# The entry of the gate-and-up stage in another order

## The chip, the core and the metric

The kernel runs on one core of one Trainium2 chip. The metric is the device time of one execution in microseconds (us), the median over several runs. TensorE (PE in the profile) multiplies, VectorE (DVE), ScalarE (ACT) and GpSimd (POOL) do the rest, and transfers are issued by the SyncE queue (SP) and by the POOL queue. The profile writes L1218 for line 1218 of the kernel.

## The reference

Two layers of a streaming encoder over 512 tokens of width 1024. Each layer is a mixer and a dense SwiGLU network, each followed by a residual and a layer norm. The change touches the second half alone, which runs once per layer:

```python
def swiglu_ffn(x, w_gate_up, w_down):
    gu = x @ w_gate_up
    gate, up = gu[..., :FFN_HIDDEN], gu[..., FFN_HIDDEN:]
    return (jax.nn.silu(gate) * up) @ w_down

x = layer_norm(DN_ALPHA * x + h, ln_g[i, 0], ln_b[i, 0])
x = layer_norm(DN_ALPHA * x + swiglu_ffn(x, w_gate_up[i], w_down[i]), ln_g[i, 1], ln_b[i, 1])
```

FFN_HIDDEN is 2816. Everything is in float32.

## The kernel before

**Split operands.** Every float32 operand is cut in two parts, a rounded one (h) and the rest (l), and a product is the sum h·h + h·l + l·h, three matmuls. `split` (L190 to L193) does it in two instructions: ScalarE rounds (`CAST`, L191), VectorE subtracts (`TENSOR_TENSOR`, L192). Each split therefore costs both engines one pass, and the matmuls with l wait for VectorE.

**Gate and up as seven products.** `ffn` (from L1121) multiplies x by the gate and up weights for six groups of 512 or 384 columns. x is seen as 2 by 2 blocks (first and second half of the tokens, first and second half of the 1024 inputs), and so are the weights (gate and up, halves of the inputs). Seven block products P1 to P7 take the place of eight, with sums of blocks on both sides. On the x side P1, P2 and P4 read blocks of x itself, and P3, P5, P6 and P7 read sums of them. `place` and `A` say where each lies: P1, P2, P4 and P7 in the tiles xh and xl, and P5, P6 and P3 in Sh and Sl.

**The sums of x.** Each token tile of 128 is turned by TensorE (`Norm.turn`, L1022) after its layer norm. The first two token tiles (t 0 and 1) are the first half: `keep` (L1153) copies what was turned into float32 tiles called full. In the first layer `again` (L1156) turns those two tiles a second time for that. The other two (t 2 and 3) are the second half: `sink` takes what was turned straight out of PSUM, and for each of them (u is 0 or 1) it makes four VectorE sums (L1177, L1179, L1180, L1184) and five splits (P3, P4, P7, P5, P6). All nine VectorE instructions and five casts are recorded inside the turn.

**The sums of the weights.** These are made by transfers that add into SBUF: `more` (L1245) issues them on the POOL queue, two of 512 KB after the splits of P1, P3, P7 and P6. P3 reads the tile Y, then a block is added to Y and P7 reads it, then another for P6, then another for P4. So P3, P7, P6 and P4 of one group form a chain: split, transfer, split, transfer. The tiles Z and those of the next groups come by the SP queue (L1241).

**A product** (`product`, L1206; its matmuls are L1218) is done in two halves of two input blocks: each half is one split of 128x1024 and twelve matmuls of 512 columns, eight with h and then four with l. The split parts go into a ring of two tiles (wh, wl). Every third half from P3 of the first group on goes into a further pair named third, made at `parts`:

```python
        if spare and count[0] % 3 == 0:
            if not third:
                third.extend(hid.make(4 + r, "third", F32R).rearrange("p m s -> p (m s)") for r in range(2))
```

It lies where `whole(1)` has its full tiles (hid 4 and 5). So the first split into third, the first half of P3 of the first group, comes after the last instruction that reads those full tiles.

**The order by hand.** `work` (L1312) sets the order of the products. G0 is the first group, G1 the second. Before the change: G0 P1 (`begin`, L1308), then the turns with their sums, then G1 P1, G0 P2, G1 P2, G0 P3, P7, P5, P6, then G0 P4, the turn of G0's first result (`turn(0)`, transposes L1296 and copies L1297), G1 P3, G0's second turn, G1 P7, P5, P6. At G0's P6 the results are combined on VectorE (`dve`, L1252): eight instructions that lead to the operand of `turn(0)`.

**What sorts the instructions.** The order of recording is not the order of running. The framework gives each engine its list: of the instructions whose inputs are ready by its own estimate of times, the one that was recorded first goes next. On the chip each list is then run strictly in turn. So the change moves recording positions, and the lists follow where readiness lets them.

**The two entries.** Layer 0 enters at L1735 to L1743 (about 415 to 484 us of the span), where turns 2 and 3 stand in the code of the body. Layer 1 enters through `down_ln` (L1036), which calls `g.between` between the last norm's scale and the last turn (about 1047 to 1115 us).

Of the kernel before, what the change touches and what calls it, by code (L numbers as in the profile page):

```python
# [13 lines left out]
ALU = mybir.AluOpType  # L14
# [3 lines left out]
P = 128  # L18
# [171 lines left out]
def split(nc, h, l, src, eng=None):  # L190
    c = nc.scalar.copy(h, src)  # L191
    (eng or nc.vector).tensor_tensor(l, in0=src, in1=h, op=ALU.subtract)  # L192
    return c  # L193
# [895 lines left out]
def run(gen):  # L1089
    while True:  # L1090
        try:
            next(gen)
        except StopIteration as e:
            return e.value
# [26 lines left out]
def ffn(g, i, hid, ep):  # L1121
# [7 lines left out]
    nc = g.nc  # L1129
# [8 lines left out]
    def place(t, S_, name):  # L1138
        return {"P1": t[:, :4, :256], "P2": t[:, 4:, :256], "P4": t[:, 4:, 256:], "P7": t[:, :4, 256:],
                "P5": S_[:, 0], "P6": S_[:, 1], "P3": S_[:, 2]}[name]  # L1140

    A = {n: (place(xh, Sh, n), place(xl, Sl, n)) for n in ("P1", "P2", "P3", "P4", "P5", "P6", "P7")}
# [3 lines left out]
    def whole(u):  # L1146
        if u not in full:
            t = [hid.make(i, "full") for i in ((4, 5) if u else (3,))]
            rows = [t[i // 3][:, i % 3] if u else t[0][:, i] for i in range(4)]
            full[u] = {n: r.rearrange("p (k t) -> p k t", t=P) for n, r in zip(("P1", "P2", "P7", "P6"), rows)}  # L1150
        return full[u]

    def keep(u, q, p):  # L1153
        nc.scalar.copy(whole(u)["P2" if q else "P1"], p)

    def again(x):  # L1156

        for u in range(2):
            for q in range(2):
# [3 lines left out]
                    nc.tensor.transpose(out=p[:, i * P:(i + 1) * P], in_=x[:, u, k * P:(k + 1) * P], identity=g.C("ident"))  # L1163
                keep(u, q, p.rearrange("p (j t) -> p j t", t=P))

    def sink(t, q, p):
        if t < 2:
            keep(t, q, p)
            return False
        u = t % 2  # L1170
        f = whole(u)

        def out(n, src):
            split(nc, *(A[n][r][:, :, P * u:P * u + P] for r in range(2)), src)

        if q == 0:
            nc.vector.tensor_tensor(f["P7"], in0=f["P1"], in1=p, op=ALU.subtract)  # L1177
        else:
            nc.vector.tensor_tensor(f["P6"], in0=p, in1=f["P7"], op=ALU.add)  # L1179
            nc.vector.tensor_tensor(f["P2"], in0=f["P6"], in1=f["P2"], op=ALU.subtract)  # L1180
            out("P3", f["P2"])
            out("P4", p)
            out("P7", f["P7"])
            nc.vector.tensor_tensor(f["P1"], in0=f["P6"], in1=f["P1"], op=ALU.subtract)  # L1184
            out("P5", f["P1"])
            out("P6", f["P6"])
        return True


    third = []  # L1190
# [110 lines left out]
    gs = [group(j) for j in range(len(GROUPS))]  # L1301
# [3 lines left out]
            for x in gs[:2]:  # L1305
                x.load(k)

    def begin():  # L1308

        gs[0].step("P1", False)  # L1310

    def work():  # L1312

        gs[1].step("P1", False)
        gs[0].step("P2", False)
        gs[1].step("P2", False)
        last = len(gs) - 1
        for j, x in enumerate(gs):
            more = j < 4
            if j:  # L1320
                if j > 1:
                    x.step("P1", more)
                gs[j - 1].step("P4", more)
                gs[j - 1].turn(0)
            x.step("P3", more)
            if j:
                gs[j - 1].turn(1)
            if j > 1:
                x.step("P2", more)
            if 0 < j < last:  # L1330
                gs[j + 1].load("Z")
                gs[j + 1].load("X")
                gs[j + 1].load("Y")
            x.step("P7", more)
            x.step("P5", more)
            x.step("P6", more)
        gs[last].step("P4", False)
        return [lambda h=h: gs[last].turn(h) for h in range(2)]
# [328 lines left out]
def body(tc, I, O, coff, voff, dbg=False):  # L1667
    nc = tc.nc
    g = Ctx()
# [3 lines left out]
    with ExitStack() as es:  # L1673
# [30 lines left out]
        def dump(n):  # L1704
            if dbg:
                nc.sync.dma_start(O[n].rearrange("(t p) d -> p t d", p=P), x)
# [3 lines left out]
        def down(hid, i, li, left, beside=None, **kw):  # L1710

            late = 4
            S_ = g.tp.tile([P, 4 * late, S], F32R, name="late")

            def rows(n, kb):
                if beside:
                    beside.step(1)
                if n == 0 and kb == 2:
                    for f in left:
                        f()  # L1720
                i_ = kb - (NH // 2 - late)
                if n and i_ >= 0:
                    hl = [(S_[:, 4 * i_ + q], S_[:, 4 * i_ + 2 + q]) for q in range(2)]
                else:
                    h, l = (g.tp.tile([P, 1024], F32R, tag=t, name=t, bufs=2) for t in ("ah", "al"))
                    hl = [(h[:, 512 * q:512 * q + 512], l[:, 512 * q:512 * q + 512]) for q in range(2)]
                for q in range(2):
                    g.copied = split(nc, *hl[q], hid.row(2 * kb + q))
                return hl

            run(down_ln(g, I[f"w_dn{i}"], NH, rows, x, li, late=late, park=hid.park, **kw))

        with tc.tile_pool(name="tp1", reuse_waits="tile", bufs=1) as tp:
            hid = Hidden(tp)
            with tc.tile_pool(name="tu1", reuse_waits="tile", bufs=1) as g.tp:  # L1735
                f = ffn(g, 0, hid, tp)
                f.load()
                f.begin()
                f.again(x)
                g.sink = f.sink  # L1740
                g.norm.turn(2)
                g.norm.scale(3)
                g.norm.turn(3)  # L1743
                g.sink = None
                dump("x0")
                left = f.work()
            with tc.tile_pool(name="td1", reuse_waits="tile", bufs=1) as g.tp:
                rope = Background(rope_tables(g))
                down(hid, 0, 1, left, rope)
                tabs = rope.finish()  # L1750
            dump("x1")
# [4 lines left out]
        with tc.tile_pool(name="tp3", reuse_waits="tile", bufs=1) as tp:  # L1756
            hid = Hidden(tp)
            with tc.tile_pool(name="tu3", reuse_waits="tile", bufs=1) as g.tp:
                f = ffn(g, 1, hid, tp)
                g.sink = f.sink  # L1760

                def places(i):
                    if i:
                        return hid.park(i - 1)
                    return [tuple(tp.tile([P, S], F32R, tag="e", name="park", bufs=10) for r in range(2)) for q in range(2)]

                g.park = places
                g.between = lambda: (f.load(), f.begin())
                run(down2)
                g.sink = None  # L1770
                dump("x2")
                left = f.work()
            with tc.tile_pool(name="td3", reuse_waits="tile", bufs=1) as g.tp:
                down(hid, 1, 3, left, final=O["out"])
# [17 lines left out]
```

## Time and profile before

| | |
|---|---|
| median of 3 runs | 1410.62 us (1406.97 to 1412.29) |
| the profiled execution | 1414.36 us, span 1412.6 us |
| TensorE matmuls busy | 1348.7 us, 95% of the span |
| VectorE busy | 950.4 us, 67% |
| ScalarE busy | 652.9 us, 46% |
| GpSimd busy | 261.2 us, 18% |
| moved by transfers | 153.46 MB |

The span is the time from the first to the last instruction in the trace. A row of the timeline gives the start, the duration, the engine and line, the tile written and the tile read, and in brackets the idle time just before it with what ended it.

### The profile page before, as it was taken

What the parts mean: (1) busy time and instruction counts of PE and PEld (TensorE: products, weight loads), DVE (VectorE), ACT (ScalarE), POOL (GpSimd) and SP (SyncE); (2) the same over time, 40 slices, a digit from 0 to 9 for tenths busy, and PEclk for the clock granted to TensorE, in tenths of its full rate; (3) what the DMA queues carried; (4) which work ended last, traced back from release to release, by engine and by line L of the source; (5) the groups of instructions that cost most, each with busy time, mean ns of one, the idle gap of its engine ahead of it and who ended that gap; (6) DMA issues with size and microseconds to landing.
All of it is one profiled execution on the core that took longest, in us unless ns stands there. A gap on an engine that the chain in (4) does not pass through costs nothing.

```text
span 1412.6 us, 21622 instructions
## 1 busy us (share of the span) xinstructions
PE 1348.7 (95%) x8382; PEld 1067.9 (76%) x8382; DVE 950.4 (67%) x1720; ACT 652.9 (46%) x1114; POOL 261.2 (18%) x276
## 2 busy tenths in 40 slices
PE   7989999999899999999999999999999999999997
PEld 4767767766577788898887877666677788997886
DVE  3588867754586677668456457888796666667556
ACT  6533234254336455455343255555545455555341
POOL 1533112322321111126401230000001111120000
PEclk9999999999899999999999999999999999999999
DMA  5212111110458698773323212121267688763232
GB/s 188 75 56 58 35 39 39 57 39 24 141 224 164 156 197 170 155 138 87 100 96 107 96 58 78 43 66 45 90 179 177 153 191 160 158 125 96 90 108 86
DMA packets 66264, 153.46 MB, mean 109 GB/s; under 512 B 20336, under 2 KB 21488, under 8 KB 66032
## 3 DMA queue, kind: packets, MB, share of 16 engines
q1 hardware_dynamic: 51808, 103.83, 22.4%
q0 software_dynamic: 13824, 46.14, 19.2%
q10 hardware_dynamic: 528, 2.10, 0.4%
q8 instruction: 66, 1.08, 0.3%
q14 instruction: 38, 0.31, 0.1%
HBM read 149.09 MB, written 2.95 MB: 108 GB/s over the span
## 4 chain that ended last, share of the span: by engine, by line
PE 66%; DVE 13%; issue 10%; DMA 6%; ACT 2%; POOL 1%; DVEq 0%; POOLq 0%; ACTq 0%; SPq 0%
PE ps_g L1218 14%; PE ps_g L185 12%; PE ps_g L186 12%; PE ps_g L187 11%; DMA raw<-in_w_gu 5%; PE ps_s L1595 3%; PE ps_o L1624 2%; PE ps_t L1611 1%; PE ps_c L696 1%; POOL raw L1245 1%; DVE x L1014 1%; DVE pr L630 1%; PE ps_c L655 1%; PE ps_c L185 1%; DVE wl L192 1%
## 5 line engine op out<-in xcount | busy, mean ns | idle before, releaser
L192 DVE TENSOR_TENSOR wl<-raw,wh 128x1024 fp32r<-128x1024 f32 (+1 forms) x116 | 127.6, 1110 | 88.1 <-ACT wh L191 86.0
L191 ACT CAST wh<-raw 128x1024 fp32r<-128x1024 f32 (+1 forms) x116 | 111.5, 965 | 139.0 <-PE ps_g L1218 93.2
L1245 POOL DMA_DIRECT2D raw<-in_w_gu x96 | 83.2, 870 | 496.8 <-DVE wl L192 398.5
L213 POOL TENSOR_TENSOR wl<-w,wh 128x512 fp32r<-128x512 f32 x64 | 89.7, 1405 | 249.0 <-ACT wh L212 201.5
L1218 PE MATMUL ps_g<-wh,xh 128*128 128x512 f32 (+1 forms) x312 | 116.6, 374 | 2.1 <-ACT wh L191 2.1
L185 PE MATMUL ps_g<-xh,wh 128*128 128x512 f32 (+2 forms) x296 | 117.1, 396 | 0.0
L1218 PE MATMUL ps_g<-wh,xl 128*128 128x512 f32 (+1 forms) x312 | 115.4, 370 | 0.0
L187 PE MATMUL ps_g<-xh,wl 128*128 128x512 f32 (+2 forms) x296 | 114.4, 386 | 0.0
L186 PE MATMUL ps_g<-xl,wh 128*128 128x512 f32 (+2 forms) x296 | 114.3, 386 | 0.0
L186 PE MATMUL ps_g<-wl,ah 128*128 128x512 f32 x288 | 112.0, 390 | 0.6 <-DVE wl L192 0.6
L185 PE MATMUL ps_g<-wh,ah 128*128 128x512 f32 x288 | 111.6, 392 | 0.8 <-ACT ah L191 0.6
L192 DVE TENSOR_TENSOR wl<-w,wh 128x1024 fp32r<-128x1024 f32 (+2 forms) x79 | 89.6, 1134 | 31.7 <-ACT wh L191 31.3
L187 PE MATMUL ps_g<-wh,al 128*128 128x512 f32 x288 | 110.8, 389 | 0.0
L191 ACT CAST wh<-w 128x1024 fp32r<-128x1024 f32 (+3 forms) x85 | 80.5, 951 | 64.0 <-PE ps_g L186 36.1
L192 DVE TENSOR_TENSOR al<-hid,ah 128x512 fp32r<-128x512 f32 x72 | 49.3, 696 | 60.5 <-ACT ah L191 60.4
L191 ACT CAST ah<-hid 128x512 fp32r<-128x512 f32 x72 | 43.5, 618 | 98.9 <-PE ps_g L186 98.9
L1218 PE MATMUL ps_g<-wh,Sh 128*128 128x512 f32 (+1 forms) x232 | 85.7, 369 | 0.0
L1218 PE MATMUL ps_g<-wh,Sl 128*128 128x512 f32 (+1 forms) x232 | 85.0, 367 | 0.0
L1218 PE MATMUL ps_g<-wl,xh 128*128 128x512 f32 (+1 forms) x312 | 78.8, 374 | 3.3 <-DVE wl L192 3.3
L212 ACT CAST wh<-w 128x512 fp32r<-128x512 f32 x64 | 39.6, 618 | 90.2 <-PE ps_g L186 56.0
L185 PEld LDWEIGHTS ps_g<-xh,wh 128*128 128x128 f32 (+1 forms) x296 | 57.0, 192 | 14.7 <-issue 5.3
L1218 PEld LDWEIGHTS ps_g<-wh,xh 128*128 128x128 f32 x312 | 59.1, 190 | 11.2 <-ACT wh L191 3.5
(458 smaller groups left out, 3266.8 us busy)
## 6 DMA issues: line engine op xcount, KB each, us to landing
raw<-in_w_gu POOLq DMA_DIRECT2D x64, 512.0 KB, 5.6
w<-in_w_dn SPq DMA_DIRECT2D x44, 512.0 KB
raw<-in_w_gu SPq DMA_DIRECT2D x32, 512.0 KB
w<-in_w_even SPq DMA_DIRECT2D x48, 256.0 KB
raw<-in_w_gu POOLq DMA_DIRECT2D x32, 384.0 KB, 4.9
w<-in_w_gu SPq DMA_DIRECT2D x12, 512.0 KB
raw<-in_w_gu SPq DMA_DIRECT2D x16, 384.0 KB
w<-in_w_q SPq DMA_DIRECT2D x12, 384.0 KB
```

Source lines behind the costliest of these rows:

```text
L185: nc.tensor.matmul(out, lhsT=wh, rhs=xh, start=first, stop=False)
L186: nc.tensor.matmul(out, lhsT=wh, rhs=xl, start=False, stop=False)
L187: nc.tensor.matmul(out, lhsT=wl, rhs=xh, start=False, stop=last)
L191: c = nc.scalar.copy(h, src)
L192: (eng or nc.vector).tensor_tensor(l, in0=src, in1=h, op=ALU.subtract)
L212: nc.scalar.copy(h, w)
L213: nc.gpsimd.tensor_tensor(l, in0=w, in1=h, op=ALU.subtract)
L630: nc.vector.tensor_tensor(pr[:, :r, :r], in0=Ti[:, :r, :r].rearrange("p s j -> p j s"), in1=bc(e.N[:, :r, r].unsqueeze(1), [64, r, r]), op ...
L1218: nc.tensor.matmul(acc[u][:, :n], lhsT=A_[a][:, k, P * u:P * u + P], rhs=w[:, q], start=first and k + a + b == 0, stop=k + b == 4, skip_gr ...
L1245: nc.gpsimd.dma_start(T[k][k2], w[r, q, k2], accum_op=ALU.add)
L1595: nc.tensor.matmul(p[:, :nk], lhsT=Q[:, h % 4, qb * P:(qb + 1) * P], rhs=K[:, h % 4, :nk], start=True, stop=True)
L1624: nc.tensor.matmul(o[64 * e:64 * e + 64, kb * P:], lhsT=Vv[:, kb, (h - 1 + e) * 64:(h + e) * 64], rhs=t[e][kb][:, kb * P:], start=kb == 0, ...
```

## The change

Three edits. In `sink`, the turn of token tiles 2 and 3 makes only what reads the transposes (sums L1177 and L1179, and the split of P4). The other two sums and four splits go to a new function `sums`, which `work` calls in two places: P3's after G0 P2, those of P7, P5 and P6 after G1 P2. Then G1 P1 is recorded earlier, between the last norm's scale and the last turn. Last, for G0 alone, `turn(0)` is recorded after G1 P3 in place of before it. No instruction is added or left out.

```diff
+    def out(u, n, src):
+        split(nc, *(A[n][r][:, :, P * u:P * u + P] for r in range(2)), src)
+
     def sink(t, q, p):
...
         if q == 0:
             nc.vector.tensor_tensor(f["P7"], in0=f["P1"], in1=p, op=ALU.subtract)
         else:
             nc.vector.tensor_tensor(f["P6"], in0=p, in1=f["P7"], op=ALU.add)
-            nc.vector.tensor_tensor(f["P2"], in0=f["P6"], in1=f["P2"], op=ALU.subtract)
-            out("P3", f["P2"])
-            out("P4", p)
-            out("P7", f["P7"])
-            nc.vector.tensor_tensor(f["P1"], in0=f["P6"], in1=f["P1"], op=ALU.subtract)
-            out("P5", f["P1"])
-            out("P6", f["P6"])
+            out(u, "P4", p)
         return True
+
+    def sums(*names):
+        for n in names:
+            for u in range(2):
+                f = whole(u)
+                o = {"P3": "P2", "P5": "P1"}.get(n, n)
+                if o != n:
+                    nc.vector.tensor_tensor(f[o], in0=f["P6"], in1=f[o], op=ALU.subtract)
+                out(u, n, f[o])
...
-    def begin():
-
-        gs[0].step("P1", False)
+    def begin(n):
+
+        gs[n].step("P1", False)

     def work():

-        gs[1].step("P1", False)
         gs[0].step("P2", False)
+        sums("P3")
         gs[1].step("P2", False)
+        sums("P7", "P5", "P6")
...
                 gs[j - 1].step("P4", more)
-                gs[j - 1].turn(0)
+                if j > 1:
+                    gs[j - 1].turn(0)
             x.step("P3", more)
             if j:
-                gs[j - 1].turn(1)
+                for h in range(0 if j == 1 else 1, 2):
+                    gs[j - 1].turn(h)
...
-                f.begin()
+                f.begin(0)
                 f.again(x)
                 g.sink = f.sink
                 g.norm.turn(2)
                 g.norm.scale(3)
+                f.begin(1)
                 g.norm.turn(3)
...
-                g.between = lambda: (f.load(), f.begin())
+                g.between = lambda: (f.load(), f.begin(0), f.begin(1))
```

## Rows read from the trace of the kernel before

**Rows 1.** The page, part 1: busy time by engine.

```profile
PE 1348.7 (95%) x8382; PEld 1067.9 (76%) x8382; DVE 950.4 (67%) x1720; ACT 652.9 (46%) x1114; POOL 261.2 (18%) x276
```

**Rows 2.** Windows: busy of PE, PEld, DVE, ACT, POOL, then PEclk, DMA share, GB/s.

```profile
430.00:435.00 5.00, 2.92 (x13) 2.06 (x11) 5.00 (x8) 3.15 (x5) 0.00 (x0) 1.00 0.84 155
...
475.00:480.00 5.00, 4.09 (x20) 3.51 (x21) 5.00 (x8) 2.17 (x4) 1.34 (x2) 1.00 0.25 43
...
1065.00:1070.00 5.00, 4.59 (x21) 3.43 (x19) 5.00 (x9) 4.27 (x7) 0.00 (x0) 1.00 1.02 311
1070.00:1075.00 5.00, 3.51 (x9) 2.79 (x10) 4.93 (x5) 3.48 (x5) 0.86 (x1) 0.70 0.42 171
```

**Rows 3.** TensorE's waits, 400 to 520 us: total, times, longest.

```profile
PE ps_g L1218 <- ACT third L191: 3.0, 2, 2.2
PE ps_s L1296 <- DVE w L1252: 2.5, 2, 1.3
```

**Rows 4.** TensorE's waits, 1030 to 1160 us.

```profile
PE ps_g L1218 <- DVE wl L192: 3.1, 3, 1.9
PE ps_s L1296 <- DVE w L1252: 1.7, 2, 1.2
PE ps_g L1218 <- ACT third L191: 1.0, 1, 1.0
```

**Rows 5.** The first entry, timeline: third's release, its split, what follows.

```profile
434.06 1.04 ACT L191 CAST third<-raw 128x1024 fp32r<-128x1024 f32 x1 [1.18 <-DVE Sl L192]
...
435.15 0.50 PE L1218 MATMUL ps_g<-third,Sh 128*128 128x512 f32 x1 [2.24 <-ACT third L191]
...
436.22 1.21 DVE L192 TENSOR_TENSOR third<-raw,third 128x1024 fp32r<-128x1024 f32 x1
...
437.96 0.86 POOL L1245 DMA_DIRECT2D raw<-in_w_gu  x1 [1.41 <-PE ps_g L1218]
...
438.49 1.21 DVE L192 TENSOR_TENSOR wl<-hid,wh 128x1024 fp32r<-128x1024 f32 x1
...
447.84 1.05 ACT L191 CAST wh<-raw 128x1024 fp32r<-128x1024 f32 x1 [3.88 <-DMA raw<-in_w_gu]
...
450.71 0.39 PE L1218 MATMUL ps_g<-wh,xh 128*128 128x512 f32 x1
```

**Rows 6.** The chain that ended last: adding transfers (start, us, what).

```profile
437.96 9.78 DMA raw<-in_w_gu
...
450.45 5.33 DMA raw<-in_w_gu
...
477.19 5.30 DMA raw<-in_w_gu
```

**Rows 7.** The first entry, timeline: from G0's results to G1's P7.

```profile
470.87 1.28 DVE L1252 TENSOR_TENSOR u<-ps_g,s 128x512 f32<-128x512 f32 x2
...
475.68 1.22 DVE L192 TENSOR_TENSOR wl<-raw,wh 128x1024 fp32r<-128x1024 f32 x1
...
482.57 1.04 ACT L191 CAST third<-raw 128x1024 fp32r<-128x1024 f32 x1 [3.81 <-DMA raw<-in_w_gu]
...
483.67 0.50 PE L1218 MATMUL ps_g<-third,xh 128*128 128x512 f32 x1 [0.78 <-ACT third L191]
```

**Rows 8.** The second entry, timeline: P2's splits, third, what follows.

```profile
1052.13 1.17 DVE L192 TENSOR_TENSOR wl<-raw,wh 128x1024 fp32r<-128x1024 f32 x1
...
1071.49 1.64 PE L1218 MATMUL ps_g<-wl,xh 128*128 128x512 f32 x4 [1.90 <-DVE wl L192]
...
1072.58 1.23 DVE L192 TENSOR_TENSOR third<-raw,third 128x1024 fp32r<-128x1024 f32 x1
...
1074.11 0.86 POOL L1245 DMA_DIRECT2D raw<-in_w_gu  x1 [11.42 <-DVE third L192]
...
1079.58 1.05 ACT L191 CAST wh<-raw 128x1024 fp32r<-128x1024 f32 x1 [1.66 <-DMA raw<-in_w_gu]
...
1082.31 0.39 PE L1218 MATMUL ps_g<-wh,xh 128*128 128x512 f32 x1
```

More of the change, by code (lines that the diff above doesn't have):

```diff
@@ L1171, in sink @@
         f = whole(u)
-        def out(n, src):
-            split(nc, *(A[n][r][:, :, P * u:P * u + P] for r in range(2)), src)
         if q == 0:
```

## The prediction

> **What bounds the kernel now.** I read the page first: TensorE's matmuls fill 95% of the span [rows 1], so time is won only where TensorE stands still. Then TensorE's waits in the two stretches that the change touches. In the first entry it waits 3.0 us for third and 2.5 us for the operand of the first turn [rows 3]; in the second 3.1 us for split weights, 1.7 us for that operand and 1.0 us for third [rows 4]. Next the windows, to see who was late: VectorE is busy for 5.00 of 5.00 us around 430 and 1065 us, and nearly so after 1070 [rows 2]. It is the engine behind there. One more loss stands in those rows: after TensorE's wait of 1.90 us [rows 8] its granted clock is 0.70 on average, between its levels of 1.2 and 2.4 GHz, so it spent part of that window at the lower. Nine matmuls take 3.51 us there, 0.39 each, against 4.59 / 21 = 0.22 in the window before [rows 2]: 9 x 0.17 = 1.5 us.
>
> Last the chain that ended last, which shows what waits behind VectorE: the adding transfers [rows 6]. A split that ends on VectorE lets POOL issue a transfer, which takes 5.3 us or, once, 9.78 us, and only then can the next product of that group be split. In G0 these links follow each other with nothing but G0's own products between.
>
> **The sums later, G1's P1 earlier.** Nothing is added or dropped; four of nine VectorE instructions per token tile are the two sums and two splits of P3 and P5, two more the splits of P7 and P6: twelve over both tiles, some 0.64 us each by the nearest pair of that size (two in 1.28 [rows 7]), move behind the splits of P2. In the first entry the wait of 2.24 us at 435.15 [rows 5] goes, since the splits of G1 P1 and G0 P2 no longer stand behind those twelve. TensorE would then reach G0 P7 at 450.71 - 2.24 = 448.47.
>
> What is late next is third. Its tiles hold the sums' inputs, so its split must follow all twelve, as its cast already followed them before [rows 5]. VectorE was full up to it, and three P2 splits ran after it (one of them is the 438.49 row [rows 5]). They are now recorded ahead of it and should run first, as the sums are no longer there to hold them up. So third's split ends at 437.43 + 3 x 1.21 = 441.06 in place of 437.43. From that end to the transfer's issue it was 0.53 us, from landing to the cast 0.10, the cast 1.05 [rows 5, 6]. With a transfer of 5.33 us G0 P7's first half is ready at 441.06 + 0.53 + 5.33 + 0.10 + 1.05 = 448.07, just ahead of TensorE at 448.47. The transfer is the unknown: its bounds are 5.30 and 9.78 [rows 6]. I take 5.33, because two of three rows lie there. The gain is 2.24 us.
>
> In the second entry the waits of 3.1 us [rows 4] and the 1.5 us of clock would go, and TensorE would be at G0 P7 at 1082.31 - 4.6 = 1077.7. But there all P2 splits ran before third already (1071.49 waits for the last but one, third follows at 1072.58 [rows 8]). VectorE has the same work ahead of third and was full, so third still ends at 1072.58 + 1.23 = 1073.81, the transfer is issued at 1074.11, and P7's cast runs from 1079.58 to 1080.63. TensorE waits 2.9 us more and starts P7 at 1080.63 in place of 1082.31: a gain of 1.68 us, with 2.9 of the 4.6 us turned into a wait for the transfer.
>
> Moves at no cost: the twelve casts (ScalarE has 3.15 of 5.00 us in use [rows 2]; if that cover went, one cast, 0.6 us). G1 P1 takes its two adding transfers with it, but the turn that it passes issues none on POOL or SP, so POOL's order stays G0 P1, G1 P1, G0 P3. Its copies go to banks of its own.
>
> **The first turn later.** The waits for its operand are 2.5 and 1.7 us [rows 3, 4]. I cost the move at nothing. VectorE makes eight combinations from 470.87 on, and only then, at 475.68, the split of G1 P3; that split's end starts the transfer at 477.19, 5.30 us, on which G1 P7 waits at 483.67 [rows 6, 7]. Moving the transposes leaves these VectorE instructions where they are, so TensorE gets G1 P3's matmuls with h earlier and then waits longer for its l parts and for P7. The bounds: both waits won, 4.2 us; or the later waits for third, 0.78 [rows 7] and 1.0 [rows 4], once more, a loss of 1.8. I take zero, as the chain through 475.68 and 477.19 is the nearest. Whatever G0 gains ahead of P6 shifts that chain as a whole, so the 2.24 and 1.68 us stay.
>
> **Sum.** 2.24 + 1.68 + 0 = 3.92 us: 1414.36 becomes 1410.4. The profiled execution lies 3.7 us above the median shown, so in medians 1410.6 becomes 1406.7.
>
> A rule against the change: adding transfers are issued by POOL while VectorE is full. The transfer at 477.19 took 5.30 us with VectorE busy for 5.00 of 5.00 us [rows 2, 6], as long as the others, so the sum charges nothing for it. The Trainium skill (SBUF — State Buffer, section Who interferes with whom) says that a VectorE instruction with two SBUF inputs contends with a GpSimd instruction that reads SBUF. By that rule each of the two transfers could stand behind one split more, an estimate of 2 x 1.2 = 2.4 us, and the sum would be a gain of 1.5; the trace does not show it.
>
> **Rivals.** (1) *All waits go.* The lists are sorted anew; where P7 is not ready, products that are (G0 P5, G1 P3) may be put ahead of it, and the turn's transposes fill the rest. Then 3.0 + 2.5 in the first entry and 3.1 + 1.7 + 1.0 + 1.5 in the second are won [rows 2 to 4], 12.8 us: 1397.8, or about 1401 with three quarters of it. For it: the list takes whatever is ready first. Against it: in both entries the order G0 P3, P7 was kept before while ScalarE stood idle 3.88 and 1.66 us for P7's transfer [rows 5, 8].
>
> (2) *The adding transfer stretches*, and the change is slower. Place: G0 P3's first half to P7. With 9.78 us as at 437.96 [rows 6], P7 is ready at 452.5 in the first entry and at 1085.1 in the second: 1.8 and 2.8 us later than before, 4.6 us in all: 1415.2. TensorE's idle time ahead of P7 would then be 4.0 and 7.4 us, far over the 1.90 us after which the clock fell, and two falls of 1.5 us make it 1418 (a fall is not certain: the 2.24 us of the first entry left the clock at 1.00 [rows 2]). It decides from a transfer of 5.33 + 2.6 = 7.9 us on in the first entry, and 5.4 + 1.7 = 7.1 in the second. For it: the 9.78 row. Against it: the two others.
>
> (3) *The order hardly changes.* The lists follow readiness: at 1052.13 the split of G1 P1 ran on VectorE although it was recorded behind both turns [rows 8]. If P2's splits find no free ring tile, VectorE takes the sums at once, as before: 1410.6.
>
> **How the numbers follow.** A measurement of this kernel can tell about 0.5%, 7 us, from no change. My forecast has 0.53; its own range is 1402.5 (the first turn's 4.2 us won as well) to 1409. Rival 1 has 0.22, rival 2 0.13, rival 3 0.12. Faster by over 0.5% (below 1403.6) is rival 1 and a tenth of the forecast: 0.27. Slower by over 0.5% is the half of rival 2 with the clock: 0.06. The same: 0.67. The range leaves out the better half of rival 1 and the worse half of rival 2: 1400 to 1414.
>
> **What would show it.** Right: no wait of TensorE between G0 P1 and G0 P3 in either entry; third's split later than 437.43 by some 3 us in the first entry and unmoved in the second; TensorE waiting for P7's cast behind a transfer near 1078 us; the wait for the first turn's operand gone and a longer one ahead of G1 P7. Wrong: P5 before P7 on TensorE (rival 1), adding transfers of 8 us and more (rival 2), or VectorE's sums still ahead of the P2 splits (rival 3). The forecast fails as a whole if the wait ahead of G1 P7 shrinks too, for then the transfers were not what set the pace.

## The result, and the profile after

The changed kernel takes 1417.71 us (median of 7 executions, 1414.6 to 1422.15) against 1411.04 before (7 executions): a ratio of 1.0051, with a 95% interval of 1.0036 to 1.0066. It is slower by some 7 us. The forecast was 1406.7 with a range up to 1414, so both the sign and the range were wrong. Rival 2 (the adding transfer stretches, 1415.2 or 1418) comes nearest. Ratios leave out single executions far slower than the rest of their kernel (one of 2634.31 us in e6_turn_back, one of 1520.11 us of the kernel before).

The page of the changed kernel: busy time by engine (part 1), and the group that P7's first matmuls belong to, all matmuls that read wh and xh (part 5).

```profile
PE 1349.3 (95%) x8382; PEld 1068.9 (75%) x8382; DVE 950.4 (67%) x1720; ACT 652.6 (46%) x1114; POOL 262.5 (19%) x276
...
L1221 PE MATMUL ps_g<-wh,xh 128*128 128x512 f32 (+1 forms) x312 | 118.0, 379 | 10.4 <-ACT wh L191 10.4
```

Part 1 is that of [rows 1] to within 1.3 us: the same work. What is new is the second line. Over the whole span TensorE stands idle 10.4 us (2.1 before) ahead of matmuls of this group, nearly all of it for ScalarE's cast. Its waits (total, times, longest) say where. First 400 to 520 us, the answer to [rows 3]:

```profile
PE ps_g L1221 <- ACT wh L191: 4.1, 2, 3.8
PE ps_g L1221 <- ACT third L191: 2.1, 1, 2.1
PE ps_s L1299 <- ACT hid L1300: 0.5, 1, 0.5
```

Then 1030 to 1160 us, the answer to [rows 4]:

```profile
PE ps_g L1221 <- ACT wh L191: 4.3, 1, 4.3
PE ps_g L1221 <- ACT third L191: 4.1, 2, 2.0
```

The waits that the change aimed at are gone: 2.24 us ahead of G0 P3 in the first entry, those of 3.1 us for split weights in the second, and those of 2.5 and 1.7 us for the first turn's operand. In their place stand one of 3.8 and one of 4.3 us ahead of G0 P7, and 2.1 and 2.0 us for third.

The timeline of the first entry, from the last sums to G0 P7, answers to [rows 5] (start, duration, engine and line, tiles, idle time before):

```profile
437.86 0.69 DVE L192 TENSOR_TENSOR Sl<-full,Sh 128x512 fp32r<-128x512 f32 x1 [0.66 <-ACT Sh L191]
...
438.82 1.23 DVE L192 TENSOR_TENSOR wl<-raw,wh 128x1024 fp32r<-128x1024 f32 x1 [0.26 <-ACT wh L191]
...
439.96 1.22 DVE L192 TENSOR_TENSOR third<-raw,third 128x1024 fp32r<-128x1024 f32 x1
440.34 0.86 POOL L1248 DMA_DIRECT2D raw<-in_w_gu  x1 [14.70 <-DVE wl L192]
441.47 0.86 POOL L1248 DMA_DIRECT2D raw<-in_w_gu  x1 [0.28 <-DVE third L192]
445.82 1.04 ACT L191 CAST third<-raw 128x1024 fp32r<-128x1024 f32 x1 [4.78 <-DMA raw<-in_w_gu]
...
448.35 1.04 ACT L191 CAST wh<-raw 128x1024 fp32r<-128x1024 f32 x1 [1.48 <-DMA raw<-in_w_gu]
...
449.44 0.79 PE L1221 MATMUL ps_g<-wh,xh 128*128 128x512 f32 x1 [3.81 <-ACT wh L191]
```

P3's second half is split first (438.82, ring tile), and its first half after it (439.96, third). The transfers follow in that order, 1.13 us apart. The first of them feeds P7's second half, whose cast starts 5.48 us after the issue; the second feeds P7's first half, and its cast starts 6.88 us after the issue. TensorE runs P7's halves in order, so the later transfer ends its wait. In the kernel before, P3's first half was split first in both entries (436.22 and 1072.58 [rows 5, 8], its second half at 443.99 and 1073.72). The second entry shows the same reversal, the answer to [rows 8]:

```profile
1073.09 1.22 DVE L192 TENSOR_TENSOR wl<-raw,wh 128x1024 fp32r<-128x1024 f32 x1
1073.70 0.50 PE L1221 MATMUL ps_g<-third,Sh 128*128 128x512 f32 x1 [2.03 <-ACT third L191]
1074.23 1.22 DVE L192 TENSOR_TENSOR third<-raw,third 128x1024 fp32r<-128x1024 f32 x1
1074.84 1.76 POOL L1248 DMA_DIRECT2D raw<-in_w_gu  x2 [13.84 <-issue]
...
1083.80 0.79 PE L1221 MATMUL ps_g<-wh,xh 128*128 128x512 f32 x1 [4.25 <-ACT wh L191]
```

The windows answer to [rows 2] (PE, PEld, DVE, ACT, POOL busy, granted clock, DMA share, GB/s). Two windows follow those around the waits, and last come the two stretches that I use from here on: from G0 P1's first matmul to G1 P5's first, once for each entry.

```profile
430.00:435.00 5.00, 5.00 (x24) 4.12 (x23) 4.89 (x8) 4.26 (x7) 0.00 (x0) 1.00 1.00 311
1065.00:1070.00 5.00, 5.00 (x24) 4.14 (x23) 5.00 (x7) 4.79 (x6) 0.00 (x0) 1.00 0.90 283
...
416.65:490.31 73.66, 66.82 (x288) 53.77 (x289) 49.84 (x59) 40.74 (x55) 12.25 (x14) 0.95 0.72 161
1047.74:1124.70 76.96, 68.06 (x300) 54.60 (x298) 53.99 (x72) 41.14 (x59) 10.37 (x12) 0.96 0.59 134
```

```profile
450.00:460.00 10.00, 10.00 (x35) 8.01 (x34) 4.33 (x4) 4.75 (x7) 1.35 (x2) 0.75 0.87 198
1080.00:1090.00 10.00, 6.20 (x15) 4.86 (x16) 4.21 (x4) 5.05 (x6) 1.73 (x2) 0.66 0.81 145
```

The same two stretches in the kernel before:

```profile
419.16:489.41 70.25, 64.51 (x288) 51.73 (x289) 48.76 (x59) 40.41 (x54) 12.25 (x14) 1.00 0.76 165
1047.44:1120.39 72.95, 67.06 (x299) 53.65 (x298) 53.30 (x72) 40.95 (x59) 10.38 (x12) 0.98 0.61 140
```

Together they are 143.20 us before and 150.62 after, 7.42 more, about what the medians differ by (6.7). The profiled executions as a whole differ by only 3.3 us of span, because that of before lost 4.1 us elsewhere (2.5 of them ahead of G0 P1, which began at 419.16, that of after at 416.65). TensorE is busy 3.3 us longer in the stretches, and idle 4.1 us longer. The longer busy time is the clock: after the two waits ahead of G0 P7 the granted clock is 0.75 and 0.66 on average, between its levels of 1.2 and 2.4 GHz, and 35 instructions stand in 10.00 us where a full window of such matmuls holds 45 or 46.

### The profile page after: what moved, and what is told of

Same layout as the page of the kernel before. It is cut to its first block, busy times and chain, and to the rows that moved or that the text cites. A ratio compares the mean times of both kernels' runs of the same rounds, so it can differ in the third digit from the quotient of the medians.

```text
span 1415.9 us, 21619 instructions
## 1 busy us (share of the span) xinstructions
PE 1349.3 (95%) x8382; PEld 1068.9 (75%) x8382; DVE 950.4 (67%) x1720; ACT 652.6 (46%) x1114; POOL 262.5 (19%) x276
## 4 chain that ended last, share of the span: by engine, by line
PE 55%; issue 18%; DVE 11%; DMA 10%; POOL 3%; ACT 2%; POOLq 0%; DVEq 0%; ACTq 0%; SPq 0%
PE ps_g L186 12%; PE ps_g L185 12%; PE ps_g L187 12%; DMA raw<-in_w_gu 9%; PE ps_s L1601 3%; PE ps_g L1221 2%; POOL raw L1248 2%; PE ps_o L1630 2%; PE ps_t L1617 1%; PE ps_c L696 1%; DVE pr L630 1%; PE ps_c L655 1%; PE ps_c L185 1%; PE ps_s L1028 1%; PE ps_c L186 1%
## 5 line engine op out<-in xcount | busy, mean ns | idle before, releaser
L1221 PE MATMUL ps_g<-wh,xh 128*128 128x512 f32 (+1 forms) x312 | 118.0, 379 | 10.4 <-ACT wh L191 10.4
```

Of the source, the lines that this page charges most:

```text
L1221: nc.tensor.matmul(acc[u][:, :n], lhsT=A_[a][:, k, P * u:P * u + P], rhs=w[:, q], start=first and k + a + b == 0, stop=k + b == 4, skip_gr ...
```

## The experiments

For every kernel I cut the two stretches at the first matmuls of G0 P7, G0 P5 and G1 P7, and add up both entries (us, one profiled execution each). The last column is the ratio to the kernel before over its executions, with a 95% interval.

| kernel | G0 P1 to P7 | G0 P7 to P5 | G0 P5 to G1 P7 | G1 P7 to P5 | sum | ratio |
|---|---|---|---|---|---|---|
| before | 66.42 | 10.88 | 54.37 | 11.53 | 143.20 | |
| after | 68.85 | 16.60 | 50.67 | 14.50 | 150.62 | 1.0051 [1.0036, 1.0066] |
| e1_sums | 68.56 | 13.99 | 53.10 | 11.40 | 147.05 | 1.0037 [1.0023, 1.0051] |
| e2_p1early | 65.05 | 11.03 | 55.01 | 11.11 | 142.20 | 0.9988 [0.9977, 0.9999] |
| e3_turn | 66.39 | 10.88 | 51.16 | 14.48 | 142.91 | 1.0036 [1.0022, 1.0051] |
| e12_turn_again | 66.40 | 10.99 | 55.57 | 16.10 | 149.06 | 1.0037 [1.0023, 1.0052] |
| e4_ring | 62.89 | 11.30 | 54.78 | 16.08 | 145.05 | 1.0018 [1.0004, 1.0033] |
| e5_fill | 69.64 | 11.01 | 55.77 | 14.48 | 150.90 | 1.0059 [1.0042, 1.0076] |
| e6_turn_back | 69.00 | 15.61 | 50.61 | 11.56 | 146.78 | 1.0033 [1.0019, 1.0046] |
| e7_p1_swap | 65.50 | 11.15 | 56.29 | 11.13 | 144.07 | 1.0006 [0.9995, 1.0018] |
| e8_swap | 63.88 | 12.84 | 56.58 | 14.50 | 147.80 | 1.0024 [1.0009, 1.0038] |
| e9_ring_back | 63.52 | 12.91 | 55.22 | 11.35 | 143.00 | 0.9982 [0.9969, 0.9996] |
| e10_ring_only | 66.30 | 11.50 | 55.88 | 11.34 | 145.02 | 1.0023 [1.0010, 1.0035] |
| e11_turn_fill | 64.80 | 10.99 | 58.13 | 17.10 | 151.02 | 1.0071 [1.0054, 1.0087] |

One execution is a rough measure: e3_turn and e12_turn_again are the same kernel, 6.15 us apart. So a verdict rests on the ratio, and the columns say where to look.

**The three edits one by one.** Theory A: the chain from third's split through the adding transfers to G0 P7 sets the pace. B: G1 P1 ahead of the last turn delays that turn and all that follows it. C: the first turn's move is what costs.

```diff
 # e1_sums: the whole change, with G1 P1 and turn(0) put back
-                f.begin(1)
...
+        gs[1].step("P1", False)
         gs[0].step("P2", False)
         sums("P3")
 # e2_p1early: the kernel before, with
+                f.begin(1)
                 g.norm.turn(3)
 # e3_turn: the kernel before, with
-                gs[j - 1].turn(0)
+                if j > 1:
+                    gs[j - 1].turn(0)
```

> The first edit alone: the two sums and four splits per token tile leave the turn and go behind the P2 products; G1 P1 and the first turn stay where they were. Theory A (the chain from third's split through the adding transfer to G0 P7 sets the pace, and all that stands ahead of that split on VectorE makes it late): third's split slips as in the changed kernel, TensorE waits 3 to 4 us ahead of G0 P7 in each entry at a lower clock afterwards; about +5 us over before. Theory B (it is G1 P1 ahead of the last turn that delays the turn, its sums and so third): no slip, 0 to -3 us. Theory C (the first turn's move is what costs): -2 to -4 us here.

> The second edit alone: G1 P1 recorded ahead of the last turn, the sums still inside the turn. Theory B: the turn of token tile 3 and all its sums come later by one product (about 5 us), third with them: +4 to +8 us, the wait ahead of G0 P7 at 3 us or more. Theory A: third's split moves little, as the same work stands ahead of it on VectorE: within 2 us of before. Theory C: within 2 us of before.

> The third edit alone: G0's first turn recorded behind G1 P3. Theories A and B: G1 P7 waits for its transfer as before, so the wait for the turn's operand (2.5 and 1.7 us) turns into a longer one ahead of G1 P7: within 2 us of before. Theory C: +5 us, with waits of 2 us and more ahead of G1 P7 and a lower clock behind them.

Against 1408.38 us before in the same runs, e1_sums took 1412.86, e2_p1early 1406.15 and e3_turn 1413.23. Edit 2 is a small gain, so B falls. Edit 1 and edit 3 each cost about 5 us, and both A and C hold in part. The three ratios add up to 1.0061, against 1.0051 for the whole.

**G0 P3 without third, and its halves in order.** Two ways to take the reversed transfers out of the whole change:

```diff
 # e4_ring: P3 of the first group in the ring (wh, wl)
-            x.step("P3", more)
+            x.step("P3", more and j > 0)
 # e8_swap: third for P3's second half, not its first
-        if spare and count[0] % 3 == 0:
+        if spare and (count[0] % 3 == 0) != (count[0] in (9, 10)):
```

> The whole change, but G0 P3's first half is split into the ring of two tiles and no longer into third, so that it need not wait for the sums' tiles. Theories A and B: its transfer goes out first and some 3 to 4 us earlier, the waits of 3.8 and 4.3 us ahead of G0 P7 and the lower clock behind them go: -8 to -12 us against the changed kernel, 1406 to 1410 where that has 1418. Theory C: within 2 us of the changed kernel.

> The whole change, and third is used for the second half of G0 P3 in place of the first; no other half changes its tiles. Theory 'reversed transfers': in the changed kernel P3's second half was split first and its transfer started first, while P7 needs the first half's transfer first. With the halves in order P7's first half is ready 1.1 to 2 us sooner in each entry, TensorE's wait ahead of it falls from 3.8 and 4.25 to 2 to 3 us and the clock holds in part: ratio 1.002, 1413. Theory 'transfers in sum' (P7 waits for whichever comes last): the wait only moves between P7's halves; ratio 1.0045 to 1.005.

e4_ring took 1410.56 us and e8_swap 1414.21, against 1408.38 and 1411.4 before in their runs. By the ratios both win back more than half of the loss of 0.0051: 0.0033 and 0.0027, though the intervals of e8_swap and of the whole change overlap a little. "Transfers in sum" falls, since 1.0045 lies outside e8_swap's interval. e4_ring fell short of its expectation (1406 to 1410 where the whole change has 1418, a ratio below 1.000). The timeline of e8_swap, first entry:

```profile
445.62 0.86 POOL L1248 DMA_DIRECT2D raw<-in_w_gu  x1 [14.69 <-DVE wl L192]
446.76 0.86 POOL L1248 DMA_DIRECT2D raw<-in_w_gu  x1 [0.28 <-DVE third L192]
451.10 1.99 ACT L191 CAST wh<-raw 128x1024 fp32r<-128x1024 f32 x2 [4.78 <-DMA raw<-in_w_gu]
...
452.20 0.50 PE L1221 MATMUL ps_g<-wh,xh 128*128 128x512 f32 x1 [1.34 <-ACT wh L191]
```

The two transfers are issued 1.14 us apart as in the changed kernel, but now the first one is P7's first half, and TensorE waits 1.34 us in place of 3.81. From G0 P1 to G0 P7 it is 30.26 us (32.79 in the changed kernel), and 33.62 in the second entry (36.06).

**The clock alone.** After the long wait matmuls run at half speed. If that were the loss, work that keeps TensorE busy through the wait would give it back:

```diff
 # e5_fill: product(), fill = 16 for G0 P3, 0 elsewhere
+        if fill:
+            p = g.pp.tile([P, S], F32, tag="s", name="ps_s", bufs=2)
+            for m in range(fill):
+                nc.tensor.matmul(p[:, :n], lhsT=A_[0][:, 0, :P], rhs=w[:, m % 2], start=True, stop=True, skip_group_check=True)
```

> The whole change, with 16 matmuls of 512 columns put between G0 P3 and G0 P7 in both entries, whose result nobody reads (operands: P3's last l part and Sh). At 0.22 us each they fill 3.5 of the 3.81 and 4.25 us in which TensorE stood idle for P7 and change nothing else. Theory 'wait' (the loss of 7 us is the time TensorE waits for the transfers): the wait is as long, only filled; ratio to before as for the whole change, 1.005, 1417. Theory 'clock' (after the long idle stretch the granted clock falls and about a dozen matmuls take 0.43 in place of 0.22 us, 2.4 and 2.8 us in the profile): the matmuls after the wait run at 0.22 us, some 5 us come back, ratio 1.0015, about 1412, and the spread between executions shrinks.

It took 1419.67 us against 1411.4: nothing came back. The filler did what it should in the first entry, as TensorE's timeline shows (16 filler matmuls, then P7, its first matmul after 0.18 us). In the second it put P7 0.77 us later, at 36.83 us from G0 P1:

```profile
448.97 3.79 PE L1226 MATMUL ps_s<-wl,Sh 128*128 128x512 f32 x16
452.94 0.50 PE L1221 MATMUL ps_g<-wh,xh 128*128 128x512 f32 x1 [0.18 <-ACT wh L191]
...
473.07 0.50 PE L1221 MATMUL ps_g<-third,xh 128*128 128x512 f32 x1 [0.78 <-ACT third L191]
...
480.27 1.20 PE L1221 MATMUL ps_g<-wl,Sh 128*128 128x512 f32 x4 [2.37 <-DVE wl L192]
```

The clock stayed up (G0 P7 to P5 took 11.01 us in place of 16.60), but 5.1 of the 5.6 us were lost again before G1 P7: 55.77 in place of 50.67. TensorE came to G0 P4 and G1 P3 sooner and waited there, 0.78 and 2.37 us in these rows. The casts of G0 P4's second half, in the changed kernel and then in e5_fill, show what took TensorE's place:

```profile
467.83 1.05 ACT L191 CAST third<-raw 128x1024 fp32r<-128x1024 f32 x1 [1.73 <-PE ps_g L1221]
```

```profile
464.53 0.86 POOL L1254 DMA_DIRECT2D raw<-in_w_gu  x1 [1.06 <-DVE wl L192]
...
471.98 1.04 ACT L191 CAST third<-raw 128x1024 fp32r<-128x1024 f32 x1 [2.79 <-DMA raw<-in_w_gu]
```

In the changed kernel it waited for TensorE, in e5_fill for the transfer behind G0 P6. That transfer was issued 1.18 us sooner, counted from G0 P1, but took 7.34 us in place of 5.50. So in this profile a faster TensorE does not bring G1 P7 forward, and neither does its clock.

What sets the pace from there on is seen in the casts. From the cast of G0 P4's second half (467.83 in the profile after) to the cast of G1 P7's first half (481.97) it took 13.7 to 14.2 us in both entries of all fourteen profiles. Between them stand that half's split, the eight combinations, G1 P3's split and one adding transfer, in this order, on VectorE and the transfer queue. In the first entry, counted from G0 P1, the first cast was at 49.48 us before, 51.18 after, 51.85 in e5_fill, 49.86 in e8_swap and 48.83 in e9_ring_back; the second at 63.41, 65.32, 65.97, 63.87 and 62.95. What is late at that first cast arrives at G1 P7, with or without a fast TensorE between. Ahead of that cast there is no such fixed length: e8_swap has G0 P7 1.29 us sooner than the kernel before and the cast 0.38 us later, in the second entry 1.25 sooner and 1.34 later. The two adding transfers behind G0 P6 lie there, and in these profiles one of them took anything from 5.1 to 7.5 us; why stays open.

**The turn.** The changed kernel with only the first turn put back, and later edit 3 alone once more, plain and filled (e11_turn_fill has the filler of e5_fill, 8 matmuls behind G1 P3):

```diff
 # e6_turn_back: the whole change, with
-                if j > 1:
-                    gs[j - 1].turn(0)
+                gs[j - 1].turn(0)
```

> The sums later and G1 P1 earlier, but G0's first turn left where it was (edits 1 and 2 without 3). Theory 'parts add up': edit 1 alone gave +5.2 and edit 2 alone -1.7 us, so +3.5, ratio 1.0025, 1414; the move of the turn then accounts for the other 3 to 4 us. Theory 'one chain' (edits 1 and 3 both only lengthen TensorE's idle stretch ahead of a P7, and the first has already spent the slack): undoing edit 3 gives back no more than 1 us, ratio 1.0045, 1417.

> Edit 3 alone once more, beside its filled version, since its first profiled execution was one of its quickest (1409.9 against a median of 1413.2): ratio 1.0035. If a slow execution is profiled: theory 'clock' sees matmuls at 0.43 us start to start after G1 P7's wait, or elsewhere in the stretch, and a stretch of 145 to 147 in place of 142.9; theory 'transposes behind the wait' sees all matmuls at 0.22 us and a stretch longer by 3 to 4 us through waits.

> Edit 3 alone, with 8 matmuls of 512 columns that nobody reads between G1 P3 and the transposes, 1.8 us in the 2.2 us in which TensorE waits for G1 P7. Theory 'clock' (edit 3 merges two idle stretches of 1.2 to 1.3 us into one of 2.2, after which the clock falls in a part of the executions: those at a mean clock of 0.981 took 1413 us and more, those at 0.983 and above 1408 to 1410): the fall goes, median 1409 to 1411, ratio 1.000 to 1.0015, against 1.0035 for edit 3 alone in the same runs. Theory 'transposes behind the wait' (the loss is TensorE work that now stands behind the wait): no gain, ratio 1.0035 or more.

e6_turn_back took 1414.98 us against 1411.4, e12_turn_again 1416.68 against 1411.64. Putting the turn back wins 0.0018 of the ratio, 2.5 us, with intervals that overlap; that of e6_turn_back holds the figures of both its theories (1.0025 and 1.0045), so the ratio alone doesn't decide between them. Moving the turn alone costs 0.0036 and 0.0037, 5 us. TensorE at G1 P7 in the changed kernel, and then in e6_turn_back:

```profile
479.94 1.03 PE L1299 MATMUL ps_s<-cst,w 128*128 128x128 f32 x8
483.06 0.50 PE L1221 MATMUL ps_g<-third,xh 128*128 128x512 f32 x1 [2.09 <-ACT third L191]
...
484.52 1.15 PE L1299 MATMUL ps_s<-cst,v 128*128 128x128 f32 x8 [0.50 <-ACT hid L1300]
```

```profile
478.63 0.60 PE L1299 MATMUL ps_s<-cst,w 128*128 128x128 f32 x4
479.56 0.63 PE L1299 MATMUL ps_s<-cst,w 128*128 128x128 f32 x4 [0.33 <-DVE w L1255]
...
485.52 1.03 PE L1299 MATMUL ps_s<-cst,v 128*128 128x128 f32 x8
487.35 0.50 PE L1221 MATMUL ps_g<-third,xh 128*128 128x512 f32 x1 [0.80 <-ACT third L191]
```

Both lists hold sixteen transposes. With the turn back, all of them lie ahead of G1 P7's first matmul, eight in the time in which VectorE makes the combinations and eight in the wait for P7's transfer. With the move, w's eight fill that wait in v's place, and v's eight fall behind it, into P7, with a wait of 0.50 us for a copy. G1 P7 to P5 takes 7.25 us in both entries in place of 5.77 and 5.79, and in every kernel with edit 3 it is 7.2 us or more. That is 1.5 us an entry, 3 in all. It is read from the place and not from a total: in e3_turn's own profile G1 P7 began 1.15 and 2.06 us sooner after G0 P5 than in the kernel before, so its sum of 142.91 is no longer than 143.20. Most of that lies ahead of the turn, as the cast of G0 P4's second half came 0.96 and 1.64 us sooner, counted from G0 P1.

The rest may be the clock. These are the windows around two waits in e3_turn, then the same in e12_turn_again, the same kernel in another execution:

```profile
430.00:440.00 10.00, 7.78 (x35) 6.12 (x34) 8.83 (x11) 6.74 (x10) 1.71 (x2) 1.00 0.67 128
480.00:490.00 10.00, 7.86 (x37) 6.29 (x38) 5.14 (x5) 8.22 (x12) 1.73 (x2) 1.00 0.81 142
```

```profile
430.00:440.00 10.00, 7.74 (x28) 5.90 (x27) 7.37 (x8) 5.79 (x8) 1.72 (x2) 0.83 0.69 140
480.00:490.00 10.00, 7.58 (x33) 5.84 (x31) 4.71 (x4) 6.91 (x10) 1.73 (x2) 0.83 0.79 139
```

The first e3 profile was a quick execution (1409.88 us, its median 1413.23), the second was at its median (1416.99, median 1416.68). The fall around 430 lies ahead of the turn's place, so the moved turn did not cause it; behind the one around 480, G1 P7 to P5 took 8.86 us in place of 7.24. The filled version was to tell the clock from the transposes and does not: its filler took one of the two PSUM tiles of the transposes, which then waited 1.8 us for copies in the first entry and 1.9 in the second. It took 1421.55 us against 1411.64. Its expectation also sorts the executions of e3_turn by clock too neatly: two at 0.984 took 1412.86 and 1414.99 us. The executions on record give an estimate instead. Within these kernels 0.001 of the mean granted clock goes with about 0.8 us. The executions of e3_turn and e12_turn_again are on average 4.35 and 4.92 us slower than those of the kernel before in their runs, at a mean clock that is lower by 0.0014 and 0.0016: about 1.0 and 1.3 us go with the clock, and 3.3 and 3.7 us are left, near the 3 us of the rows above.

**Third in other company.** Edit 2 with P3's halves swapped as in e8_swap, and the kernel before with the line of e4_ring:

> Edit 2 alone (G1 P1 earlier, ratio 0.9988 when run alone), and third is used for the second half of G0 P3 in place of the first; no other half changes its tiles. Theory 'third holds the chain': the first half of P3 needs no tile that the sums read, so its transfer starts when its own split is done and the waits for third and P7 in the first entry (2.1 + 1.2 us) go in part: ratio 0.997, 1406. Theory 'VectorE full' (whichever half is split first, VectorE has the twelve sums and splits ahead of it): no change beyond edit 2, ratio 0.9985 to 1.000.

> The kernel before with one change: G0 P3 in the ring in place of third; the sums stay inside the turns. Theory 'third alone' (the wait of 2.24 us at G0 P3 was for third's tiles, not for the sums' place): the wait goes without moving any sum, stretch 141 to 142, ratio 0.9985. Theory 'VectorE in order' (VectorE is full and the splits come in the same order, whichever tile they write): the wait moves to the split of the ring tile, stretch 143, ratio 1.000.

Neither helps. e7_p1_swap took 1411.23 us against 1411.4, a ratio of 1.0006 where edit 2 alone had 0.9988. e10_ring_only took 1414.35 against 1411.64 and lost 2.7 us, which neither theory foresaw. Its waits, 400 to 520 us, the longest of them in the timeline, and the cast of P3's first half:

```profile
PE ps_g L1218 <- DVE wl L192: 2.5, 2, 2.3
```

```profile
435.36 2.33 PE L1218 MATMUL ps_g<-wl,xh 128*128 128x512 f32 x8 [2.28 <-DVE wl L192]
...
442.89 1.05 ACT L191 CAST wh<-raw 128x1024 fp32r<-128x1024 f32 x1
...
452.09 0.50 PE L1218 MATMUL ps_g<-wh,xh 128*128 128x512 f32 x1 [0.79 <-ACT wh L191]
```

The matmuls that wait 2.28 us read xh, so they aren't P3's (which read Sh): they are the l parts of G1 P1's second half and of G0 P2's first. In the kernel before TensorE's list had one matmul of third just ahead of these, and the wait of 2.24 us was put down to it:

```profile
433.95 1.21 DVE L192 TENSOR_TENSOR wl<-raw,wh 128x1024 fp32r<-128x1024 f32 x1
...
435.49 1.09 PE L1218 MATMUL ps_g<-wl,xh 128*128 128x512 f32 x4
```

But that split of G1 P1 ended at 435.16, when the wait ended (435.15). So the wait was for G1 P1's split behind the sums as much as for third, and it stays when P3 is split into the ring. What the ring cost in the first entry is seen in the other rows: P3's first half was cast at 442.89 in place of 434.06, and G0 P7 began 1.23 us later, counted from G0 P1. The second entry shows no such loss (33.52 for 34.87), so where the 2.7 us lie over many executions stays open.

**Both repairs together.** The sums later, G1 P1 earlier, G0 P3 in the ring, the turn where it was:

> Edits 1 and 2 with the first turn left where it was, and G0 P3 in the ring (wh, wl) in place of third. I count the stretch from G0 P1's to G1 P5's first matmul in the profile, summed over both entries: 143.2 us before, 150.6 with the whole change, 146.8 without the turn's move, 145.1 with the whole change and P3 in the ring. Theory 'two separate losses' (third holds G0 P7's transfers; the turn's move puts eight transposes behind a wait in place of ahead of it): both fall away, 145.1 - 3.8 = 141.3, 2 us better than before: ratio 0.9985, 1408.5. Theory 'one chain': as one of them alone, 145, ratio 1.002.

1409.16 us against 1411.64, ratio 0.9982 [0.9969, 0.9996], where 0.9985 was expected; the whole change has 1.0051. This is 2.5 us quicker than the kernel before. It cannot be told from edit 2 alone (0.9988), so of the sums' move no gain of its own is shown. Its own profiled execution has stretches of 143.00 us where 141.3 was expected, no shorter than before, so the single profile doesn't show this gain; the ratio over 11 executions does. In that profile G0 P7 starts 1.12 and 1.78 us sooner than in the kernel before, but the cast of G0 P4's second half comes only 0.65 us sooner in the first entry and 0.37 later in the second.

## Why the prediction was wrong, step by step

From 139.3 us forecast for the two stretches (143.2 - 3.92) to 150.62 measured it is 11.3 us. By parts, first and second entry: G0 P7 starts 3.48 and 2.87 us later than forecast (32.79 for 29.31 and 36.06 for 33.19, from G0 P1), the clock after it costs 2.73 and 2.99, the transposes behind G1 P7 1.51 and 1.46; between G0 P5 and G1 P7 2.07 and 1.63 come back, because TensorE was late and had less to wait for. Some of that goes with the second transfer behind G0 P6, which took 5.50 and 5.37 us in place of 6.80 and 6.39.

**Right: the waits ahead of G0 P3 in the first entry go.** TensorE is busy for 5.00 of 5.00 us around 430, and it was ready for G0 P7 at 449.44 - 3.81 = 445.63, which is 28.98 after G0 P1 (forecast 29.31). The reason given, splits behind the sums, holds too; by e10_ring_only the 2.24 us were as much a wait for G1 P1's split as for third. In the second entry the waits for split weights went, but one of 2.03 us for third took their place (1073.70), which the sum did not have.

**Wrong: "third's split ends at 441.06".** From G0 P1 that is 21.90; it ended at 441.18, which is 24.53 from a G0 P1 that began 2.51 us earlier. I counted three P2 splits ahead of it and left out P3's own second half (1.14 us from start to start), which writes a ring tile, needs none of the sums and was ready first. VectorE also stood idle 0.66 and 0.26 us for casts in the rows above, and for less at three places before (its splits at 423.26 and 428.70, its sum at 430.63). Compared with starts that follow each other without a gap, the five come to 1.7 us, while the three P2 splits took 0.2 less than 3 x 1.21; with the 1.14 that makes the 2.6 us between 21.90 and 24.53. The moved casts that I held for free were bounded at 0.6 (and they are eight, not twelve: four of the twelve VectorE instructions are sums without a cast). In the second entry the split ended at 1075.45, 1.34 later than forecast from G0 P1; again 1.14 of it is the second half.

**Wrong: "a transfer of 5.33 us".** It took 6.85 in the first entry and 6.94 in the second. The change put two transfers 1.13 and 0.90 us apart, with the needed one second. The trace of before held such a pair, in the second entry, in rows that the prediction did not read (issue, then the cast behind it):

```profile
1075.24 0.86 POOL L1245 DMA_DIRECT2D raw<-in_w_gu  x1 [0.28 <-DVE wl L192]
...
1082.15 1.05 ACT L191 CAST third<-raw 128x1024 fp32r<-128x1024 f32 x1 [1.52 <-DMA raw<-in_w_gu]
```

This one was issued 1.13 us after the transfer of 1074.11 [rows 8] and took 6.81 us, the first of the two 5.39; there the needed one went first. Nor were "two of three rows" a fair sample: of the 29 adding transfers issued in the kernel before between 410 and 495 and between 1040 and 1130 us, 13 took over 6 us. Of the 3.88 us by which P7's first half was ready later than forecast in the first entry (32.79 against 28.91 us from G0 P1), the reversed order of P3's halves makes 1.14 + 1.52 = 2.66. e8_swap, where the needed transfer goes first, has G0 P7 at 30.26 and 33.62, 2.53 and 2.44 us sooner than the changed kernel, and within a microsecond of what this step had forecast (29.31 and 33.19). So the step failed mainly by the order of two halves of one product.

**Wrong: "I cost the move at nothing", the first turn.** The reason given was right: the chain through G1 P3's split and its transfer kept its length, and the waits for w's operand won nothing. But the text held that TensorE then only "waits longer". It did not follow the eight v transposes, which had filled that wait and now stand behind it. The bound of 1.8 us for both entries had the sign and was too small: 3.0 us, and by the estimate above some 1 us of clock on top.

**Right in part: "Whatever G0 gains ahead of P6 shifts that chain as a whole".** From the cast of G0 P4's second half on the chain keeps its length, for losses too, and in e5_fill a TensorE that came sooner did not make them good. But what is gained at G0 P7 need not reach that cast, as e8_swap and e9_ring_back show, so the 2.24 and 1.68 us would not have been safe even with the halves in order.

**Rival 2** had the place (G0 P3 to P7), the idle time (4.0 us forecast in the first entry, 3.81 measured; 7.4 and 4.25 in the second) and, with the clock, the time (1418). Its condition was one transfer of 7.1 to 7.9 us; what came was 6.85 together with a split that ended later. At 0.13, with half of it for the clock, it was given too little. Rival 1 did not come: G0 P7 kept its place ahead of P5. Rival 3 did not either, since the P2 splits did move ahead.

**The rule weighed against the change.** The transfer at 441.47 was long while VectorE was busy for only 2.98 us of the window from 440 to 450. VectorE ran a single instruction while it was under way (446.90, 1.23 us) and none while POOL issued it. What the Trainium skill states in SBUF — State Buffer, section Who interferes with whom, of VectorE against GpSimd can't be what lengthened it; no run here shows that contention.

## What to carry to other kernels

When a split or a sum is moved later, list again everything on that queue which becomes ready sooner than it, the other half of the same product above all: a list that takes what is ready first can reverse two transfers whose consumer needs them in order. When TensorE waits for a chain of transfers, work that lies in that wait is free and the same work behind it is not, so a moved turn is charged by what falls out of the wait. And before a gain on TensorE is booked, follow the chain to the next point where TensorE waits; if filling TensorE's idle time with dead work does not change the total, its clock and its idle time are symptoms. Read every transfer of the kind that the sum uses, not the few on the chain that ended last: here a pair like the one that made the loss stood in the trace of before.

## What the runs showed of the hardware

**Two adding transfers close together.** Of a pair of 512 KB issued 0.9 to 1.1 us apart the first took, from issue to landing, 5.38 and 5.22 us in the changed kernel's two entries, 5.46 and 5.40 in e8_swap and 5.39 in the second entry of the kernel before; the second took 6.85 and 6.94, 6.93 and 7.03, and 6.81. With 1.55 and 1.74 us between the issues, in e9_ring_back, the second took 6.47 and 6.25. A wider gap alone does not make them short: in the kernel before the two behind G0 P6, issued at 458.48 and 461.74, took 6.87 and 6.80, and the one of 437.96 took 9.78 [rows 6]. What lengthened these was not tested.

**The clock falls after the same wait in one execution and not in the next.** At G0 P3 TensorE waited 2.22 us in e3_turn and the granted clock of the window was 1.00; in e12_turn_again, the same kernel, it waited 2.26 us and the clock was 0.83, seven matmuls fewer in the window. In the kernel before, 2.24 us left it at 1.00, and 1.90 us brought 0.70 over 5 us [rows 2]. Over the executions of one kernel the time follows the mean granted clock: of the seven of the changed kernel the quickest had 0.983 (1414.6 us) and the slowest 0.976 (1422.15). Its median is 0.980, that of the kernel before 0.984. Giving the clock back does not by itself give the time back: e5_fill has the clock of the kernel before (median 0.984) and is as slow as the whole change.
